# Products of probabilities and values: the second head of a pair asked for first in each part

## The chip, the cores and the metric

The kernel runs on one core of a Trainium2 chip. The metric is the device time of one execution in microseconds (us). TensorE does the matrix products (PE in the profile's lines, with PEld for its loads of the stationary operand), VectorE is DVE, ScalarE is ACT, GpSimd is POOL and SyncE is SP.

## What is computed

One layer of a decoder with 256 tokens and a model width of 2048, all in float32: a norm, one input projection that feeds three kinds of attention (dilated windows "a", block-sparse "b", and "c" with compressed, selected and window branches), the output projection, a second norm, and a feed-forward block with a short convolution. What the change touches is the last step of every attention head, the product of its probabilities with its values:

```python
p, lse = masked_softmax(s, mask)
o = jnp.einsum('bdhnqk,bdhnke->bdhnqe', p.astype(v.dtype), vb)          # mixer a
o_s = jnp.einsum('bkgqs,bkqse->bkgqe', p_s.astype(v_slc.dtype), vs)     # mixer c, selected
o_w = jnp.einsum('bkgqs,bkse->bkgqe', p_w.astype(v_win.dtype), vw)      # mixer c, window
return g[..., 0:1] * o_c + g[..., 1:2] * o_s + g[..., 2:3] * o_w
```

There are 12 heads in a, 8 in b and 12 in c, each 64 wide. In c every head has a selected and a window branch with probabilities of their own, so there are 44 sets of probabilities in all.

## The kernel before

**Stages.** First come the input projections (`fm_unit` and `tm_group`), with the attention mixed in, then the output projection (the loops from L690 and L701), then the up projection (L751, 88 units) and the down projection (L765). Weights come from memory by SyncE's queue (L120); ScalarE makes their high part `wh` (L122) and VectorE the rest `wl` (L124). `product` multiplies both with the activations on TensorE: L182 streams 512 columns with `wh`, L186 streams 256 columns with `wl`.

**Attention as side work.** Each kind of attention is a Python generator. `step()` (L651) advances it between pieces of the projections, so the program order mixes both. That order is not yet the order on the engines: the kernel is built with `schedule_with_timeline_sim=True` (L861), and a planner then puts each engine's instructions into an order of its own, by program order and by its own estimates of when each operand will be there. Instructions that write the same tile keep their program order in it.

**One set of probabilities** (`pipeline`, L595). `scores` (L502) is on TensorE and `softmax` (L516) on VectorE and ScalarE; `scale` (L554) multiplies by the factors; `turn` (L558) transposes three blocks on TensorE (L560 to L562) into `pt`, and ScalarE copies them to `pts` (L564). After every second set, `values(a, b)` (L566) is called for the pair: `a` is the first and `b` the second head, and the turn of `a` stands ahead of that of `b` in the program.

**The pair's products** (`values`). Both heads write one PSUM tile `o`: `a` its partitions 0 to 63, `b` its partitions 64 to 127 (`half`, L304). The stationary operand is a block of values of 64 columns, which the trace shows as `128*64`, while projections and transposes are `128*128`. In a and b a pair has three parts of 128 columns. In c it has two parts, of 128 and 256 columns, for each of the two branches; the first branch starts `o` with a product of the compressed branch (L572), the second ends it. Each `T.matmul` in float32 at L580 or L572 shows as two loads and two matmuls in the trace. In all there are 22 calls: 12 in c, 6 in a, 4 in b. When a tile is complete, `keep` (L584) copies it out (L591, L592) and frees `o`, of which there is one.

In what follows a0, a1 (and a2) are the parts of the first head, b0, b1 (and b2) those of the second.

Of the kernel before, what the change touches and what calls it, by code (L numbers as in the profile page):

```python
# [89 lines left out]
def trunk(ctx, tc, xT, wfm, wtm, wout, wup, wdown, w1, w2, pe, relT, convp, onehot, maskc, cmask, vbmask, out):  # L90
# [116 lines left out]
    with tc.tile_pool(name="sc", bufs=2, space=bass.MemoryType.PSUM) as scp, \  # L207
# [96 lines left out]
        def half(i):  # L304
            return slice(64 * i, 64 * i + 64)
# [260 lines left out]
        def values(a, b):  # L566

            if st.get("o") is None:
                st["o"] = opp.tile([P, 512], F32, name="o")
                if a.group in "sw":  # L570
                    p = (a.h - 20) // 2
                    T.matmul(st["o"][:, :S], cmp["vb"][p // 4][:, p % 4, :], cmp["pc"][p // 4], start=True, stop=False)  # L572
            lo, hi = slice(0, P), slice(P, S)
            if a.group in "sw":
                parts = ((1, hi, slice(S, 384), False, False), (0, slice(0, S), slice(0, S), False, a.group == "w"))
            else:
                parts = ((0, hi, hi, True, False), (1, hi, slice(S, 384), False, True), (0, lo, lo, True, True))
            for kt, cols, src, start, stop in parts:
                for n in (a, b):
                    T.matmul(st["o"][half(n.hf), cols], vt[n.v][:, kt, n.col:n.col + HD], n.ts[:, src], start=start, stop=stop)  # L580
            if b.done is not None:
                keep(b.done)

        def keep(tile_i):  # L584
            o = st["o"]
            if 6 <= tile_i < 10:
                t = ap.tile([P, 2, S], F32R, name=f"ob{tile_i}", tag=("vc", "va0", "va1", "ob")[tile_i - 6])
            else:
                t = oo[0][:, tile_i if tile_i < 6 else tile_i - 4]
            oparts[tile_i] = t  # L590
            A.copy(t[:, 0, :], o[:, :S])  # L591
            V.tensor_tensor(t[:, 1, :], o[:, :S], t[:, 0, :].bitcast(F32), ALU.subtract)  # L592
            st["o"] = None

        def pipeline(insts, late, after):  # L595

            n = len(insts)
            for j in range(n + late + 2):
                ahead(insts, j)
                i = j - late - 1  # L600
                if 0 <= i < n and i % 2 == 1:
                    values(insts[i - 1], insts[i])
                if 0 <= j - late < n:
                    turn(insts[j - late])
                if j < n:
                    scores(insts[j])
                    softmax(insts[j])
                    after(j)
                yield
# [91 lines left out]
        for o in range(NK):  # L701
# [3 lines left out]
            for i in range(4):  # L705
                a, b = (t[:, (o % 2 * 4 + i) * P:(o % 2 * 4 + i + 1) * P] for t in w)
# [10 lines left out]
    for o in range(NK):  # L717
        for c in range(0, NF, 8):
            n = min(8, NF - c)
# [3 lines left out]
    with tc.tile_pool(name="act", bufs=1) as fp, tc.tile_pool(name="frot", bufs=2) as rp, \  # L723
# [41 lines left out]
        for o in range(NK):  # L765
            ps = fps.tile([P, 512], F32, name="up")
            for c in range(0, NF, 8):
                n = min(8, NF - c)
# [105 lines left out]
```

## Time and profile before

| what | us |
|---|---|
| median of three runs | 1191.85 |
| lowest and highest run | 1191.47 and 1200.58 |
| the profiled execution | 1195.29 |
| span of its instructions | 1193.5 |

The profiled execution took 1.8 us more than its span. The page of the profile gives busy times of the engines, groups of instructions and waits. The timeline lists instructions in order of time: the start, how long the row lasts, engine, line, operation, output and inputs, shapes and the number of merged instructions. Matmuls overlap in it, so the distance from one start to the next is what a matmul costs.

### The profile page before, as it was taken

Reading aid. Unit: us, or ns where it says so; the run is one execution under the profiler, and the core shown is the slowest. Engines: PE = TensorE matmul, PEld = TensorE weight load, DVE = VectorE, ACT = ScalarE, POOL = GpSimd, SP = SyncE. Lnnn points to the kernel's source line nnn. Section 1 sums busy time; section 2 is a strip of 40 time slices with the busy share of each in tenths; the row PEclk is TensorE's granted clock in tenths of the full one; section 3 lists DMA queues with packets and bytes.
Section 4 is the critical chain, followed back from the end, with each engine's and each line's share of the span. In section 5 each row is a group of like instructions: output and inputs, shape, how many; then the busy total and the mean of one; then the engine's idle time right before and its main releaser. Section 6 shows DMA issues by size and latency. Waiting matters only on the chain.

```text
span 1193.5 us, 18698 instructions
## 1 busy us (share of the span) xinstructions
PE 1168.9 (98%) x6874; PEld 1022.8 (86%) x6874; DVE 862.4 (72%) x1635; ACT 670.6 (56%) x1153; POOL 83.6 (7%) x105
## 2 busy tenths in 40 slices
PE   7999999999999999999999999999999999999996
PEld 6898888888888898888888888888888888888886
DVE  7867987767686696888888878878878655454443
ACT  6465787766774455655556555555555544444441
POOL 7400000100000090000000000000000000000000
PEclk9989999999999998999999999999999999999998
DMA  8575445556455754555555555555555666666661
GB/s 263 176 241 183 126 125 158 139 177 199 149 164 150 220 169 166 193 192 188 187 193 190 184 192 191 187 189 192 188 190 187 182 184 184 188 184 191 186 185 71
DMA packets 66795, 214.91 MB, mean 180 GB/s; under 512 B 7584, under 2 KB 10416, under 8 KB 66704
## 3 DMA queue, kind: packets, MB, share of 16 engines
q1 hardware_dynamic: 64896, 209.19, 54.8%
q0 software_dynamic: 1808, 4.53, 2.0%
q8 instruction: 54, 0.88, 0.3%
q14 instruction: 37, 0.30, 0.1%
HBM read 211.55 MB, written 2.15 MB: 179 GB/s over the span
## 4 chain that ended last, share of the span: by engine, by line
PE 91%; POOL 5%; DMA 2%; DVE 1%; issue 0%; ACT 0%; SPq 0%; DVEq 0%; POOLq 0%
PE up L182 39%; PE up L186 20%; PE mm L182 12%; PE mm L186 6%; PE o L580 2%; PE mm L386 2%; PE mm L385 2%; PE mm L387 2%; POOL ssq L242 1%; POOL ssq L170 1%; POOL sq L168 1%; PE sc L509 1%; DMA w1t<-in_w_dram 1%; DMA raw<-in_wfm_dram 1%; PE pt L560 1%; DMA gx<-in_xT_dram 1%
## 5 line engine op out<-in xcount | busy, mean ns | idle before, releaser
L124 DVE TENSOR_TENSOR wl<-raw,wh 128x1024 fp32r<-128x1024 f32 (+4 forms) x411 | 485.8, 1184 | 196.2 <-ACT wh L122 187.5
L122 ACT CAST wh<-raw 128x1024 fp32r<-128x1024 f32 (+4 forms) x411 | 411.2, 1001 | 284.8 <-PE up L182 192.5
L182 PE MATMUL up<-xx,wh 128*128 128x512 f32 x1408 | 486.2, 394 | 0.0
L186 PE MATMUL up<-xx,wl 128*128 128x256 f32 x1408 | 380.8, 281 | 0.0
L182 PEld LDWEIGHTS up<-xx,wh 128*128 128x128 f32 x1408 | 259.1, 188 | 51.4
L186 PEld LDWEIGHTS up<-xx,wl 128*128 128x128 f32 x1408 | 266.5, 189 | 7.9
L182 PE MATMUL up<-aa,wh 128*128 128x512 f32 x660 | 230.7, 393 | 0.0
L186 PE MATMUL up<-aa,wl 128*128 128x256 f32 x660 | 184.1, 283 | 0.0
L182 PE MATMUL mm<-xx,wh 128*128 128x512 f32 x448 | 161.5, 400 | 4.5 <-ACT wh L122 4.5
L182 PEld LDWEIGHTS up<-aa,wh 128*128 128x128 f32 x660 | 123.0, 188 | 27.3
L186 PE MATMUL mm<-xx,wl 128*128 128x256 f32 x448 | 124.6, 288 | 3.7 <-DVE wl L124 3.7
L186 PEld LDWEIGHTS up<-aa,wl 128*128 128x128 f32 x660 | 124.1, 188 | 1.4
L203 ACT COPY low<-up 128x256 f32<-128x256 f32 x88 | 32.7, 372 | 130.0 <-PE up L182 127.3
L182 PEld LDWEIGHTS mm<-xx,wh 128*128 128x128 f32 x448 | 84.0, 190 | 19.8 <-ACT wh L122 4.5
L186 PEld LDWEIGHTS mm<-xx,wl 128*128 128x128 f32 x448 | 85.5, 191 | 7.9 <-DVE wl L124 4.9
L204 DVE TENSOR_TENSOR low<-up,low 128x256 f32<-128x256 f32 x88 | 37.3, 424 | 57.0 <-ACT low L203 57.0
L182 PE MATMUL mm<-oo,wh 128*128 128x512 f32 x192 | 67.7, 399 | 0.0
L738 ACT ACTIVATE acc<-u,cw 128x256 f32<-128x256 f32 x88 | 53.2, 605 | 3.3 <-DVE u L736 0.6
L186 PE MATMUL mm<-oo,wl 128*128 128x256 f32 x192 | 52.0, 284 | 0.0
L386 PE MATMUL mm<-wh,xx 128*128 128x384 f32 (+2 forms) x128 | 46.2, 361 | 0.0
L387 PE MATMUL mm<-wl,xx 128*128 128x384 f32 (+2 forms) x128 | 46.1, 362 | 0.0
L385 PE MATMUL mm<-wh,xx 128*128 128x384 f32 (+2 forms) x128 | 46.0, 360 | 0.0
(206 smaller groups left out, 1263.6 us busy)
## 6 DMA issues: line engine op xcount, KB each, us to landing
raw<-in_wup_dram SPq DMA_DIRECT2D x176, 512.0 KB, 4.1
raw<-in_wdown_dram SPq DMA_DIRECT2D x80, 512.0 KB, 3.7
raw<-in_wfm_dram SPq DMA_DIRECT2D x62, 512.0 KB, 4.5
raw<-in_wo_dram SPq DMA_DIRECT2D x32, 384.0 KB, 3.1
raw<-in_wtm_dram SPq DMA_DIRECT2D x16, 384.0 KB, 3.5
bias<-table POOLq DMA_DIRECT2D x32, 128.0 KB, 3.7
raw<-in_wtm_dram SPq DMA_DIRECT2D x8, 512.0 KB, 4.5
raw<-in_wo_dram SPq DMA_DIRECT2D x8, 512.0 KB, 4.2
```

Of the source, the lines that this page charges most:

```text
L122: A.copy(wh[:, :n], raw[:, :n])
L124: V.tensor_tensor(wl[:, :n], raw[:, :n], wh[:, :n].bitcast(F32), ALU.subtract)
L168: G.tensor_tensor(tmp, x[:, o, :], x[:, o, :], ALU.mult)
L182: T.matmul(ps, a, m.rearrange("p c s -> p (c s)"), start=start, stop=stop)
L186: T.matmul(ps[:, :S], b, m[:, 0, :], start=False, stop=False)
L203: A.copy(t, ps[:, S:])
L204: V.tensor_tensor(t, ps[:, :S], t, ALU.add)
L385: T.matmul(pss[tt][:, :n], xx[:, kt, 0, ts], a, start=kt == 0, stop=False)
L386: T.matmul(pss[tt][:, :n], xx[:, kt, 1, ts], a, start=False, stop=False)
L387: T.matmul(pss[tt][:, :n], xx[:, kt, 0, ts], b, start=False, stop=kt == NK - 1)
L580: T.matmul(st["o"][half(n.hf), cols], vt[n.v][:, kt, n.col:n.col + HD], n.ts[:, src], start=start, stop=stop)
L738: A.activation(acc, u[:, 2:], AF.Identity, bias=cw[:, n, 3:4], scale=cw[:, n, 0:1])
```

## The change

In each part of `values`, the product of the second head `b` is written ahead of that of the first head `a`. Nothing is added or removed; the operands, the flags and the number of instructions stay.

```diff
@@ -576,7 +576,7 @@
             else:
                 parts = ((0, hi, hi, True, False), (1, hi, slice(S, 384), False, True), (0, lo, lo, True, True))
             for kt, cols, src, start, stop in parts:
-                for n in (a, b):
+                for n in (b, a):
                     T.matmul(st["o"][half(n.hf), cols], vt[n.v][:, kt, n.col:n.col + HD], n.ts[:, src], start=start, stop=stop)
             if b.done is not None:
                 keep(b.done)
```

## Rows read from the trace of the kernel before

**Rows 1.** The page, busy time of each engine, its share and instructions.

```profile
PE 1168.9 (98%) x6874; PEld 1022.8 (86%) x6874; DVE 862.4 (72%) x1635; ACT 670.6 (56%) x1153; POOL 83.6 (7%) x105
```

**Rows 2.** Busy time in three stretches: length, engines, PE's clock, DMA share, GB/s.

```profile
0.00:85.00 85.00, 74.28 (x399) 65.35 (x400) 64.31 (x92) 49.38 (x86) 36.53 (x42) 0.96 0.70 229
85.00:400.00 315.00, 315.00 (x1922) 268.66 (x1921) 240.02 (x716) 207.08 (x468) 15.56 (x29) 1.00 0.54 158
400.00:1193.50 793.50, 779.64 (x4557) 688.83 (x4555) 558.04 (x828) 414.12 (x600) 31.50 (x34) 0.99 0.57 183
```

**Rows 3.** Waits of PE: line, releaser, us in total, times, longest.

```profile
PE mm L186 <- DVE wl L124: 3.7, 4, 1.6
PE mm L146 <- POOL ssq L170: 2.7, 1, 2.7
```

**Rows 4.** Source line L580: loads for b (ns least/median/most), idle load path before all.

```profile
L580 PEld LDWEIGHTS o<-pts,v_b x48: 132/137/138, 350.3 to 372.3; 128*64 128x64 f32 x48
...
issue: 5.6, 21
```

**Rows 5.** Timeline of PE, a pair of b whose products stand in two places.

```profile
357.94 0.40 PE L182 MATMUL mm<-oo,wh 128*128 128x512 f32 x1
358.27 0.43 PE L580 MATMUL o<-pts,v_b 128*64 128x128 f32 x2
358.63 0.33 PE L560 MATMUL pt<-ident,p 128*128 128x128 f32 x1
...
359.37 0.28 PE L186 MATMUL mm<-oo,wl 128*128 128x256 f32 x1
359.58 0.87 PE L580 MATMUL o<-pts,v_b 128*64 128x128 f32 x10
360.38 0.50 PE L182 MATMUL mm<-oo,wh 128*128 128x512 f32 x1
```

**Rows 6.** Timeline of PE, the last pair of b, in one place, after projection products.

```profile
371.37 0.40 PE L182 MATMUL mm<-oo,wh 128*128 128x512 f32 x1
371.60 0.28 PE L186 MATMUL mm<-oo,wl 128*128 128x256 f32 x1
371.81 0.88 PE L580 MATMUL o<-pts,v_b 128*64 128x128 f32 x12
372.62 0.50 PE L182 MATMUL mm<-oo,wh 128*128 128x512 f32 x1
```

**Rows 7.** Timeline of PE, window branches of c: second stretch of one pair, another pair whole.

```profile
149.73 0.86 PE L580 MATMUL o<-pts,v_c 128*64 128x128 f32 x6
150.53 0.38 PE L507 MATMUL sc<-k,q 128*128 128x256 f32 x1
...
185.27 0.87 PE L580 MATMUL o<-pts,v_c 128*64 128x128 f32 x8
186.07 0.33 PE L560 MATMUL pt<-ident,p 128*128 128x128 f32 x1
```

**Rows 8.** Timeline of PE, c's selected branch: L572 by itself, and ahead of its pair.

```profile
137.22 0.59 PE L572 MATMUL o<-cvals 128*128 128x256 f32 x2
137.65 0.27 PE L560 MATMUL pt<-ident,p 128*128 128x128 f32 x1
...
156.68 0.60 PE L572 MATMUL o<-cvals 128*128 128x256 f32 x2
157.21 0.87 PE L580 MATMUL o<-pts,v_c 128*64 128x128 f32 x8
158.01 0.38 PE L507 MATMUL sc<-k,q 128*128 128x256 f32 x1
```

**Rows 9.** Timeline of ACT, the copy of the second head's probabilities for rows 5.

```profile
355.81 0.46 ACT L564 COPY pts<-pt 128x384 f32<-128x384 f32 x1
```

**Rows 10.** First and last short stretch of L580 but those of rows 5, PE's timeline.

```profile
138.30 0.43 PE L580 MATMUL o<-pts,v_c 128*64 128x128 f32 x2
...
365.31 0.43 PE L580 MATMUL o<-pts,v_b 128*64 128x128 f32 x2
```

## Prediction

> **What bounds the kernel now.** I read the page's first section, then the busy times by stretch, then PE's waits. PE is busy for 98% of the span [rows 1], but a busy PE is not a bound by itself, so the stretches count. [...] PE's idle time lies at the start (10.7 of the first 85 us) and behind 400 us (13.9 of 793.5) [rows 2]. Its waits for `wl` come to 3.7 us in four times and, as PE is never idle between 85 and 400 us, none of them is there [rows 3]. So from 85 to 400 us every 0.1 us that PE's stream loses or gains moves all that follows: what is shortened there must show in the end, unless it opens a wait.
>
> The next question is what L580 costs PE in that stretch. The source view of the line shows that the load path stood idle before L580's loads, for 5.6 us in 21 places under "issue" alone [rows 4]. The timeline tells why. From one L182 to the next instruction is usually 0.23 us (371.37 to 371.60) [rows 6]. From an L182 to an L580 behind it, it is 0.33 (357.94 to 358.27) [rows 5], so 0.10 us go on entering the form `128*64`. A stretch of two L580 instructions then takes 0.36 us to the next instruction (358.27 to 358.63), but a stretch of ten only 0.80 (359.58 to 360.38) [rows 5] and one of twelve 0.81 (371.81 to 372.62) [rows 6]. A stretch has a fixed price, and in a long one the two halves of the columns run side by side.
>
> **Which pairs stand in two places.** In rows 5 the two instructions at 358.27 are a0 alone, and the ten at 359.58 are b0, a1, b1, a2, b2. In rows 6 all twelve are together. I went through the timeline of the 22 pairs: 13 have a0 alone, at 138.3, 146.1, 158.4, 170.1, 191.8 (behind an L572), 202.8, 211.2 (likewise) and 217.9 us in c, at 248.2 and 301.8 in a, and at 350.3, 358.3 and 365.3 in b; the other 9 are whole. The first and the last short stretch beside rows 5 are in [rows 10], and all but the two behind an L572 look the same. That makes 22 + 13 = 35 stretches of L580.
>
> The planner causes this, not the chip: at 358.27 the probabilities of the second head had long been copied (355.81 + 0.46 = 356.27) [rows 9]. In the planner's own estimate a0 can go and b0 can't yet; so it issues a0, then other products, then b0 and all that stands behind it in the tile's program order.
>
> **The change part by part.** It removes no instruction and no DMA: 216 matmuls at L580 before and after, and no queue of SP or POOL gets another order by the text of the change.
>
> 1. *b0 becomes the head of the pair.* It needs the later probabilities, and a0 stands behind it in the order of `o`. So a0 can no longer go early, and when b0 goes, the copy for a0 lies behind it in time too. The 13 short stretches go.
> 2. *Price of one short stretch:* 0.36 us and 0.10 for entering = 0.46 us.
> 3. *What the moved product costs in its new place.* In b and a the stretch of ten becomes one of twelve: 0.80 against 0.81 us [rows 5, 6]. In c's window branch the stretch of six becomes one of eight: 0.80 (149.73 to 150.53) against 0.80 (185.27 to 186.07) [rows 7]. So it costs 0.01 us at most by these rows; I take 0.01. They show the same work with `a` in front; with `b` in front the halves only change places. If a0 did not run beside anything, the bound would be the two loads it brings, 2 x 0.137 = 0.27 us [rows 4]; the other bound is 0. I take the end that the rows show.
> 4. *L572.* In c's selected branch it stays first and needs neither head's probabilities, so it may now be issued early and stand alone in any of the six selected pairs. Alone it takes 0.43 us to the next instruction (137.22 to 137.65) and the pair then enters anew for 0.10, 0.53 in all; in front of its pair it is 0.53 (156.68 to 157.21) [rows 5, 8]. I take nothing. The last two pairs of c read 64 rows in it, without a row of a lone one; by the price of one short stretch each way, two of them can't move the sum by more than 0.9 us, which the range holds.
> 5. *What is late next.* a0 ends later, but the last product of a pair, which releases `keep`, stands where it stood. The wait for b0 is not new: b0 headed the second stretch before, and in rows 5 its probabilities were there 3.3 us before its start (356.27 to 359.58) [rows 5, 9]. Behind b0 in PE's queue stand the projection products, so a late b0 would hold them all; that is the rival below.
>
> The sum: 13 x (0.46 - 0.01) = 5.9 us off PE's stream, 3.6 of it in c, 0.9 in a and 1.4 in b. The weights must follow: DVE needs 240.0 us for what would then take 309.1 instead of 315 [rows 2], 78% instead of 76%, which leaves it room. Behind 400 us the squares on POOL (L170) hold PE for 2.7 us [rows 3], but they begin only when the output projection's sums are there, so they move with PE.
>
> [...]
>
> **The rivals.**
>
> *A. The moved product is paid in its new place.* Each pair gains 0.46 - 0.27 = 0.19 us, 13 x 0.19 = 2.5 us: 1189.4 us on the median. Against it stand the equal stretches of rows 5 to 7; for it only that no row shows `b` in front. [...]
>
> *B. The change does not do what it says.* The planner could part the pair elsewhere, after b0 say, when its estimate of the next product is late. Then 13 stretches come back in another form, and the time stays at 1191.9 us. Against it: behind b0 no pair is parted now; the rest is always in one piece.
>
> *C. b0 holds PE (slower).* With a0 gone from the front there is nothing of the pair to run while the second copy is awaited. If the planner's order brought b0 so early that PE waited for one copy of 0.46 us [rows 9] in each of 22 pairs, the loss would be 10.1 us, and 1191.9 - 5.9 + 10.1 = 1196.1 us the time. It decides from 0.27 us of waiting per pair (5.9 / 22). Against it: the margin is 3.3 us in rows 5.
>
> *D. The planner's whole order shifts.* Where one product moves, its estimates of everything behind move, and transposes, scores and weight splits can change places. A worse order could add waits like the 3.7 us for `wl` [rows 3], which gives 1186.0 + 3.7 = 1189.7, twice that 1193.4; a better one could take as much off, 1182.3 or less. Nothing in the rows tells the sign; PE without any idle time and DVE at 76% speak for small effects.
>
> **How the numbers follow.** The profiled execution took 1195.29 us, 1.8 around its span of 1193.5 included; there the sum gives 1189.4. The median of the runs is 3.4 us below it, and the gain doesn't hang on what sets these runs apart: 1191.85 - 5.9 = 1186.0 us. Chances: the forecast 0.70 (1184 to 1188), A 0.07, B 0.07, C 0.04, D to the worse 0.07 and to the better 0.05. The range reaches from 1181, below D's better case, to 1192.5, which takes in A, B and the first step of D; about 0.1 is left out, at C and the far ends of D. About 1% (12 us) is what a measurement of this kernel can tell from no change; the forecast of 0.5% lies within it. Faster by over 1% (below 1179.9) needs D twice over, 0.04; slower by over 1% (above 1203.8) needs C with twice its stall or D at its worst, 0.03; within 1% 0.93.
>
> **What would show it right or wrong.** In the timeline after, no stretch of two L580 instructions stands alone, and there are 22 stretches instead of 35, of 8 or 12 instructions each. In the source view of L580 the idle time under "issue" and its count fall by about a third. PE's idle time from 85 to 400 us stays at nothing, and the work of that stretch ends about 5.9 us earlier, with what follows as long as before. Long stretches of 1.0 us or more to the next instruction would show A; short ones left over would show B; waits of L580 for `pts` L564 in PE's idle time would show C; new waits for `wh`, `wl` or other tiles would show D, and then the prediction is wrong by their sum.

## The result

| | before | after |
|---|---|---|
| median of 20 runs, us | 1196.57 | 1190.35 |
| lowest and highest, us | 1191.47 and 1202.69 | 1185.33 and 1193.95 |
| profiled execution, us | 1195.29 | 1189.61 |

The ratio of after to before is 0.9942 (95% interval 0.9929 to 0.9954): 0.6% or 6.9 us faster (the two medians lie 6.2 us apart). That is clear of the noise of 20 runs, although the prediction took about 1% for what a measurement of this kernel can tell from no change.

The busy times of after in the same stretches as [rows 2] (length, PE, PEld, DVE, ACT, POOL, clock, DMA share, GB/s):

```profile
0.00:85.00 85.00, 74.68 (x383) 65.82 (x384) 62.97 (x91) 48.52 (x85) 36.86 (x42) 0.92 0.71 229
85.00:400.00 315.00, 315.00 (x1960) 272.80 (x1959) 242.72 (x721) 210.21 (x471) 15.55 (x29) 1.00 0.56 161
400.00:1187.90 787.90, 773.96 (x4535) 683.97 (x4533) 555.89 (x824) 412.57 (x598) 31.49 (x34) 0.99 0.57 184
```

PE is still never idle from 85 to 400 us, and more instructions fit in: 1960 instead of 1922. DVE is at 77%. The three longest waits of PE in after (line, releaser, us, times, longest) are below. The first, for the first weights, was 4.5 us in before; the other two stand in [rows 3]. As PE is never idle between 85 and 400 us, no wait lies there:

```profile
PE mm L182 <- ACT wh L122: 4.4, 1, 4.4
PE mm L186 <- DVE wl L124: 3.1, 3, 1.4
PE mm L146 <- POOL ssq L170: 2.7, 1, 2.7
```

The pair that is the third of b, in after's timeline of PE. In before it stood in two places, at 365.3 [rows 10] and 366.6 us:

```profile
363.38 0.28 PE L186 MATMUL mm<-oo,wl 128*128 128x256 f32 x1
363.59 0.88 PE L580 MATMUL o<-pts,v_b 128*64 128x128 f32 x12
364.40 0.33 PE L560 MATMUL pt<-ident,p 128*128 128x128 f32 x1
```

All twelve instructions are in one place, 0.81 us to the next instruction, as for the whole pair in [rows 6]. After's timeline has 22 stretches of L580, twelve of 8 and ten of 12 instructions, and no short one. The source view of L580 in after, idle time of the load path before its loads (us, times):

```profile
issue: 2.7, 10
ACT pts L564: 0.8, 3
```

With five single ones behind these there are 18 places and 4.6 us, where before had 33 places and 8.7 us, "issue" in [rows 4] among them. "issue" alone fell by half, and not by the third that was forecast. The three places under `pts` are not waits for the copies: by the timelines of ACT and PE the second head's copy had ended at least 2.9 us before the start of each of the 22 stretches.

**Where the time went.** Two points can be found in every trace: the 153rd L186, which lies ahead of the first scores (L507), and the first L191, in the output projection's second loop. Between them lies all that the change touches: ahead of the first point and behind the second, PE's instructions come in the same order of lines in before, in after and in every kernel of the experiments. PE's timeline, first of before, then of after:

```profile
99.48 0.28 PE L186 MATMUL mm<-xx,wl 128*128 128x256 f32 x1
...
413.29 0.28 PE L191 MATMUL mm<-ob,wh 128*128 128x256 f32 x1
```

```profile
102.29 0.28 PE L186 MATMUL mm<-xx,wl 128*128 128x256 f32 x1
...
409.41 0.28 PE L191 MATMUL mm<-ob,wh 128*128 128x256 f32 x1
```

The stage took 313.81 us before and 307.12 after: 6.7 us less. The rest of the profiled difference is not the change's. After reached the first point 2.8 us later, and what follows the second was 1.7 us shorter (780.2 to 778.5). At both places PE's granted clock was 0.50 for a while, for a length that differs between executions: ahead of the first point for 6.8 us in before and for 3.4 and 10.2 us in after, near 450 us for 6.8 us in before and for 3.4 in after. The mean clock in the two stretches, of before, then of after:

```profile
40.00:90.00 50.00, 47.62 (x267) 43.44 (x266) 35.25 (x71) 30.48 (x57) 5.66 (x7) 0.93 0.66 216
...
440.00:460.00 20.00, 17.28 (x85) 14.88 (x84) 11.06 (x15) 8.90 (x11) 9.42 (x12) 0.83 0.50 169
```

```profile
40.00:90.00 50.00, 47.76 (x249) 43.51 (x248) 32.14 (x60) 29.20 (x56) 5.22 (x7) 0.86 0.62 205
...
440.00:460.00 20.00, 17.29 (x92) 14.98 (x92) 10.92 (x17) 8.82 (x11) 5.78 (x9) 0.91 0.57 185
```

50 x 0.07 = 3.5 us lost and 20 x 0.08 = 1.6 us won by the clock are near the 2.8 and 1.7. So 2.8 - 6.7 - 1.7 = -5.6 us, the difference of the spans.

### The profile page after: what moved, and what is told of

It reads as the page before. It is cut to its first block, busy times and chain, and to the rows that moved or that the text cites. A ratio compares the mean times of both kernels' runs of the same rounds, so it can differ in the third digit from the quotient of the medians.

```text
span 1187.9 us, 18694 instructions
## 1 busy us (share of the span) xinstructions
PE 1163.6 (98%) x6874; PEld 1022.6 (86%) x6874; DVE 861.6 (73%) x1635; ACT 671.3 (57%) x1153; POOL 83.9 (7%) x105
## 4 chain that ended last, share of the span: by engine, by line
PE 91%; POOL 5%; DMA 2%; DVE 1%; issue 0%; ACT 0%; SPq 0%; DVEq 0%; POOLq 0%
PE up L182 40%; PE up L186 20%; PE mm L182 12%; PE mm L186 6%; PE mm L387 2%; PE mm L385 2%; PE mm L386 2%; PE o L580 1%; POOL ssq L242 1%; POOL ssq L170 1%; POOL sq L168 1%; PE sc L509 1%; DMA w1t<-in_w_dram 1%; DMA raw<-in_wfm_dram 1%; PE pt L422 1%; PE pt L560 1%
## 5 line engine op out<-in xcount | busy, mean ns | idle before, releaser
L186 PE MATMUL up<-xx,wl 128*128 128x256 f32 x1408 | 380.2, 280 | 0.0
L186 PEld LDWEIGHTS up<-xx,wl 128*128 128x128 f32 x1408 | 266.0, 189 | 7.9
L186 PE MATMUL up<-aa,wl 128*128 128x256 f32 x660 | 184.1, 283 | 0.0
L186 PE MATMUL mm<-xx,wl 128*128 128x256 f32 x448 | 125.2, 289 | 3.1 <-DVE wl L124 3.1
L186 PEld LDWEIGHTS up<-aa,wl 128*128 128x128 f32 x660 | 124.1, 188 | 1.4
L186 PEld LDWEIGHTS mm<-xx,wl 128*128 128x128 f32 x448 | 86.5, 193 | 7.0 <-DVE wl L124 4.4
L186 PE MATMUL mm<-oo,wl 128*128 128x256 f32 x192 | 51.7, 282 | 0.0
```

The costliest lines, as they stand in the source:

```text
L186: T.matmul(ps[:, :S], b, m[:, 0, :], start=False, stop=False)
```

## Experiments

The theory is that of places: each separate stretch of L580 has a price on PE, and the time follows their number. Its rivals are that the order of the halves is worth something in itself, and that the planner's other moves made the gain. Seven kernels tell them apart. Since the clock at the start moves a run by some us (2.8 between the two profiled executions above), three measures stand side by side in the table: the stage between the two points in the profiled execution; the median over runs of span times mean granted clock (the length at full clock, if all work slowed with it), less 1181.6 us, its value in 50 runs of before; and the ratio of times with its interval (20 runs of the change, 6 of together and of together_all, 10 to 12 of the others).

| kernel | stretches of L580 | stage against before, us | span x clock against before, us | ratio (95%) |
|---|---|---|---|---|
| before | 35 | 0 | 0 | 1 |
| the change | 22 | -6.69 | -6.5 | 0.9942 (0.9929 to 0.9954) |
| swap_c | 27 | -3.93 | -3.5 | 0.9983 (0.9971 to 0.9995) |
| swap_ab | 30 | -2.66 | -2.1 | 0.9986 (0.9968 to 1.0004) |
| turn_b_first | 22 | -5.45 | -6.6 | 0.9964 (0.9949 to 0.9979) |
| turn_b_first_swap | 36 | +0.57 | +1.1 | 0.9999 (0.9985 to 1.0013) |
| heads_apart | 22 | -4.20 | -4.2 | 0.9973 (0.9957 to 0.9988) |
| together | 16 | -8.70 | -8.7 | 0.9935 (0.9911 to 0.9960) |
| together_all | 12 | -10.04 | -10.0 | 0.9912 (0.9890 to 0.9935) |

### The change in c alone, and in a and b alone

```diff
-                for n in (b, a):
+                for n in (b, a) if a.group in "sw" else (a, b):
```

Expected of swap_c: 

> The second head stands first only in c (12 of the 22 calls); a and b keep the order of before. Theory of places: the time follows the number of separate stretches of L580 on TensorE. The order built here has 27 (35 before, 22 after the change), all 8 short ones of c are gone, and the 6.7 us that TensorE's stream gained between the first attention work and the end of the output projection come to 0.51 us for each of the 13: 8 x 0.51 = 4.1 us faster than before, a ratio near 0.9966. Rival of the halves (it is the order of the two column halves itself that is worth something, in each call): 12/22 x 6.9 = 3.8 us, hardly to be told apart by time here. Rival of a shifted order (the gain comes from other work that the planner moved): no tie to 8 of 13, so anything from 0 to 7 us.

```diff
-                for n in (b, a):
+                for n in (a, b) if a.group in "sw" else (b, a):
```

Expected of swap_ab: 

> The second head stands first only in a and b (10 of the 22 calls). Theory of places: 30 stretches of L580 in the order built, 5 fewer than before: 5 x 0.51 = 2.6 us faster than before, a ratio near 0.9979, and with the run of c alone the two gains add up to that of the whole change. Halves: 10/22 x 6.9 = 3.1 us. Shifted order: no tie, and the two gains need not add up.

The two points, in PE's timeline of swap_c, then of swap_ab:

```profile
105.87 0.28 PE L186 MATMUL mm<-xx,wl 128*128 128x256 f32 x1
...
415.75 0.28 PE L191 MATMUL mm<-ob,wh 128*128 128x256 f32 x1
```

```profile
101.26 0.28 PE L186 MATMUL mm<-xx,wl 128*128 128x256 f32 x1
...
412.40 0.28 PE L191 MATMUL mm<-ob,wh 128*128 128x256 f32 x1
```

309.88 and 311.14 us: 3.93 us less than before for 8 stretches fewer, 2.66 less for 5, so 0.49 and 0.53 us for each, against 0.51 for the whole change. Both add up to 6.59 of 6.69 us. By span times clock the gains are 3.5 and 2.1 us, which add up to 5.6 of 6.5. The ratios say less: 0.17% and 0.14% add up to about half of the change's 0.58%; the interval of swap_c leaves out the 0.9966 of the theory by a little, and that of swap_ab holds 1. The profiled execution of swap_c reached the first point 6.4 us later than that of before, in work that no edit touches. A shifted order has no reason to add up like this in the stage; the halves are not excluded yet.

### Which head's probabilities come last

```diff
-                if 0 <= j - late < n:
-                    turn(insts[j - late])
+                if 0 <= j - late < n and (j - late) % 2 == 1:
+                    turn(insts[j - late])
+                    turn(insts[j - late - 1])
```

Expected of turn_b_first, this edit on the kernel before: 

> The products keep the order of before (first head first), but the turns of a pair are swapped: both in the second head's step, the second head's ahead of the first's, so that the first head's probabilities now come last. Theory of places: the head of the pair waits for the last probabilities, as in the change, and the order built has 22 stretches: about 13 x 0.51 = 6.7 us faster than before, a ratio near 0.9944, with 1 to 2 us to either side for the later turn of the first head. Halves: the second head is not in front, so the time of before, ratio 1.000. Shifted order: no tie to the 6.7.

Expected of turn_b_first_swap, this edit on the changed kernel: 

> The turns of a pair are swapped as in the run before, and the products too, as in the change: the second head is in front again, but its probabilities now come first. Theory of places: the head of the pair goes early by itself; the order built has 36 stretches, 14 of them short: 0.5 us slower than before, a ratio near 1.0004, and 7.2 us slower than the run with the turns alone. Halves: the gain of the change stays, ratio near 0.994. Shifted order: no tie.

The two points in turn_b_first, then in turn_b_first_swap:

```profile
106.29 0.28 PE L186 MATMUL mm<-xx,wl 128*128 128x256 f32 x1
...
414.65 0.28 PE L191 MATMUL mm<-ob,wh 128*128 128x256 f32 x1
```

```profile
103.14 0.28 PE L186 MATMUL mm<-xx,wl 128*128 128x256 f32 x1
...
417.52 0.28 PE L191 MATMUL mm<-ob,wh 128*128 128x256 f32 x1
```

308.36 and 314.38 us. With the order of before, but the first head's probabilities last, the stretches fall to 22 and the gain comes, although `b` is nowhere in front. Its stage holds one loss of its own, a piece at low clock (turn_b_first, busy times by stretch):

```profile
126.00:130.00 4.00, 4.00 (x17) 3.55 (x16) 2.27 (x6) 0.00 (x0) 0.00 (x0) 0.57 0.46 153
```

4 x (1 - 0.57) = 1.7 us; without it the stage would be 7.2 us shorter than before. The ratio of times, 0.9964 (0.9949 to 0.9979), stays behind the 0.9944 of the theory; the mean granted clock of its runs is lower than that of before's (0.9875 against 0.9887), and by span times clock the gain is 6.6 us. With `b` in front and its probabilities first, 14 short stretches come back and the gain is gone: +0.57 us in the stage, 0.9999 in time. The theory of the halves, which wanted 1.000 and 0.994 here, falls. So does that of a lucky order: of the stage's 1696 instructions outside L580, about 1540 keep before's order in the change, 1370 in turn_b_first and 1430 in turn_b_first_swap, and the time follows the stretches.

### How far the halves run side by side

```diff
-            for kt, cols, src, start, stop in parts:
-                for n in (b, a):
+            for n in (b, a):
+                for kt, cols, src, start, stop in parts:
```

Expected of heads_apart: 

> The change, but with all parts of the second head written ahead of all parts of the first, so the two column halves no longer take turns in the program order. The order built has 22 stretches of L580, as with the change, so the theory of places alone gives the change's time. What is tested is how far the halves run side by side. If they do so only for neighbours in the order, a pair of a or b takes about 0.16 + 10 x 0.109 + 0.20 = 1.45 us instead of 0.81 and one of c some 0.5 us more than its 0.80: 10 x 0.64 + 12 x 0.5 = 12.4 us slower than the change, 5.7 us slower than before, a ratio near 1.005. If each half has its own way through the array whatever the order (or if they never ran side by side), the change's time stays, a ratio near 0.994, and the stretches stay at 0.80 us to the next instruction.

A pair of b and a pair of c in PE's timeline of heads_apart:

```profile
352.54 1.14 PE L580 MATMUL o<-pts,v_b 128*64 128x128 f32 x12
353.62 0.50 PE L182 MATMUL mm<-oo,wh 128*128 128x512 f32 x1
...
145.40 0.88 PE L580 MATMUL o<-pts,v_c 128*64 128x128 f32 x8
146.21 0.38 PE L507 MATMUL sc<-k,q 128*128 128x256 f32 x1
```

Neither theory had it. In c the four instructions of one head stand ahead of the four of the other, and a stretch still takes 0.81 us: its first two instructions start 13 ns apart, against 7 ns in the change. The records don't name the half of an instruction; it is inferred here from the order that the program asks for and from the spacing of the starts. In a and b six stand ahead of six, and a stretch takes 1.08 us instead of 0.81: two instructions run alone (from 352.54 and from 352.70 us), and only at 352.81 do two start together. 10 x 0.27 = 2.7 us, and the stage is 2.5 us longer than the change's. So the halves do run side by side beyond their neighbours, but only up to some distance, between four and six instructions here; and had they never done so, every stretch would be longer than 0.81 (1.45 us for one of twelve, by the estimate in the expectation).

### Fewer places still

In together, the selected branch's products of a pair of c wait for those of the window branch and follow them:

```diff
...
-                    values(insts[i - 1], insts[i])
+                    if insts[i].group == "s":
+                        held.append((insts[i - 1], insts[i]))
+                    else:
+                        values(insts[i - 1], insts[i], *held)
+                        held.clear()
...
-            for kt, cols, src, start, stop in parts:
-                for n in (b, a):
...
+            for pair in ((a, b),) + more:
+                for kt, cols, src, start, stop in parts:
...
+                    for n in pair[::-1]:
...
-            n.ts = rp.tile([P, 384], F32, name="pts", bufs=4)
+            n.ts = rp.tile([P, 384], F32, name="pts", bufs=6)
```

Expected of together: 

> The change, and in c the products of a pair's selected branch are held back and issued behind those of its window branch, in one place, with six buffers for the turned probabilities instead of four. The order built has 16 stretches, 6 fewer than the change. Theory of places: 6 x 0.51 = 3.1 us faster than the change, 19 x 0.51 = 9.7 us faster than before, a ratio near 0.992. Rival of held buffers: the selected branch's probabilities stay longer in their buffers and the tile o is copied out later by one stretch; if turns or projections wait for that, the gain is lost and TensorE shows waits between 85 and 400 us.

In together_all the test also holds back the first of two pairs of a or b; the second is then written to columns 0 to 255 of `o`, the one held back to columns 256 to 511:

```diff
-                    if insts[i].group == "s":
+                    if insts[i].group == "s" or insts[i].group in "ab" and i % 4 == 1 and i + 2 < n:
```

Expected of together_all: 

> As the run named together, and in a and b every two pairs of heads share one tile o (columns 0 to 255 and 256 to 511), so that their products stand in one place too, the later pair's first. The order built has 12 stretches, 10 fewer than the change. Theory of places: 10 x 0.51 = 5.1 us faster than the change, 23 x 0.51 = 11.7 us faster than before, a ratio near 0.990. Rival of held buffers: what is held longer (probabilities, the tile o until two copies are out) opens waits on TensorE, and the time falls short of that of the run named together or comes out above it.

The two points in together, then those of together_all with two of its pairs of b in one place (the product has line L585 there):

```profile
100.90 0.28 PE L186 MATMUL mm<-xx,wl 128*128 128x256 f32 x1
...
406.00 0.28 PE L191 MATMUL mm<-ob,wh 128*128 128x256 f32 x1
```

```profile
98.67 0.28 PE L186 MATMUL mm<-xx,wl 128*128 128x256 f32 x1
...
361.31 1.53 PE L585 MATMUL o<-pts,v_b 128*64 128x128 f32 x24
362.77 0.39 PE L186 MATMUL mm<-oo,wl 128*128 128x256 f32 x1
...
402.44 0.28 PE L191 MATMUL mm<-ob,wh 128*128 128x256 f32 x1
```

305.10 and 303.77 us. Both are faster than the change in the stage, by 2.0 us for 6 stretches and by 3.3 us for 10, where 3.1 and 5.1 were expected. No wait was opened: PE is busy for 315 of 315 us from 85 to 400 us in both. The price was mis-sized instead, since 0.51 us is that of a short stretch, and those were gone. A short stretch is also work that runs beside nothing: its two instructions start 0.16 us apart, where those of a whole stretch start in pairs, 7 ns apart. Two whole stretches of twelve take 2 x 0.81 = 1.62 us, one of twenty-four 1.46 (361.31 to 362.77); with one way in (0.10) and one way out (0.10, below) less, that is 0.36 us, and 10 x 0.36 = 3.6 us, near the 3.3. together_all has the best time of all, in six runs: 0.9912 of before, with an interval that overlaps the change's at its edge (0.9929 to 0.9935); the stage of the profiled execution and span times clock put it 3.3 and 3.5 us below the change.

## Why the prediction was right

**The bound.** PE's stream from 85 to 400 us set the time, and what was taken from it showed at the end: 6.7 us of the stage, 6.9 by the ratio.

**b0 as head, the 13 short stretches.** As forecast: all are gone, and 22 are left. turn_b_first shows that this, and not the place of the halves, is the cause; swap_c and swap_ab show it in parts. What the planner estimated, no run shows; the traces show the orders that it built.

**The price of one.** The mechanism was right and the size a little low, 0.45 us forecast against 0.51. The term that was missing is the way out: the first product behind a stretch is longer too. Before's timeline, behind the short stretches at 138.30 [rows 10] and 358.27 [rows 5]:

```profile
138.66 0.39 PE L186 MATMUL mm<-xx,wl 128*128 128x256 f32 x1
138.88 0.40 PE L182 MATMUL mm<-xx,wh 128*128 128x512 f32 x1
...
358.80 0.27 PE L561 MATMUL pt<-ident,p 128*128 128x128 f32 x1
358.91 0.27 PE L562 MATMUL pt<-ident,p 128*128 128x128 f32 x1
```

The L186 there takes 0.22 us to the next instruction; the usual one, over all of before's attention, takes 0.12. L560 takes 0.17 (358.63 to 358.80), its neighbour L561 0.11. Of the 13 short stretches 8 are followed by another product and 5 by L560: 8 x 0.10 + 5 x 0.06 = 1.1 us. The sum would have been 7.0 us, 0.3 above the 6.7 measured. The step that failed is item 2, which counted the way into the form `128*64` and the stretch, but not the way back.

**The moved product.** Free, as taken from the rows: the stretches keep 0.80 and 0.81 us with `b` in front. Rival A, which wanted 0.27 us more in each, falls; heads_apart adds that the halves stay side by side even when they are not neighbours. Both halves use all 128 rows, and their twelve instructions take 0.81 us, half of what the twelve loads alone would take one behind the other (12 x 0.137 = 1.64 us, by the median load in [rows 4]).

**L572.** Nothing, as taken: its 12 instructions and the way to the next take 3.26 us in before's stage and 3.25 in after's, summed from start to start, though two more of its pairs stand alone now.

**What is late next.** No wait for the copies (rival C): the least time between a second head's copy and the stretch that needs it was 2.9 us. No new wait for weights or other tiles (rival D), no pair parted in a new way (rival B).

**The time itself.** 1186.0 was forecast and 1190.35 measured. That lies outside the 1184 to 1188 to which the prediction gave 0.70, and nearer to the times of rival A (1189.4) and of rival D (1189.7); it is the trace, and not the time, that tells them apart. The miss has little to do with the change: the three runs of before that the forecast started from lay low (1191.85 against 1196.57 for 20), which is 4.7 us and more than the whole miss. From 1196.57 the same sum gives 1190.7. The forecast's own ratio, 0.9951, is 0.0009 above the measured one. That the profiled execution took 1189.61 us, where the sum gave 1189.4, is luck: the stage gave 0.8 us more than the sum, and what lies outside it took 1.1 us back (2.8 - 1.7).

## What to carry to other kernels

Where small products in another tile form are scattered through a stream that bounds the kernel, count the places (0.51 us for each short one here) and not the instructions, and read the price of a place from start to start, the way in and the way out included. Where a planner builds the order, an operand that is ready early can cause such a place (36 stretches in turn_b_first_swap, 22 in turn_b_first); to ask first for the one that comes last keeps the group together, here at no cost that the trace shows. A gain of this size is best read between two points of the trace that enclose it, with the granted clock between them beside it, and not from whole runs.

## What was not expected of the hardware

By the starts in heads_apart the two halves of 64 columns seem to have taken their matmuls out of program order: with four instructions of one half written ahead of four of the other they started 13 ns apart, with six ahead of six the second half started two instructions late. No run tells what sets this distance.

The clock made up most of the spread between runs. In the traces of before and after, PE's granted clock fell to 0.50 behind idle times near the start and near 440 us, for the lengths given above, and in turn_b_first inside a stage without idle time (0.57 from 126 to 130 us). The profiled executions of swap_ab and together had a mean clock of 0.992 over the span, against 0.990 in before and in after, though the load path waited for L170 in them as long as in before or longer (3.0 and 3.3 us against 3.0). Span times mean granted clock spread little: over 33 runs of before its mean is 1181.6 us with a standard deviation of 0.8 (a standard error of 0.13), while their times go from 1192.4 to 1202.3 with a standard deviation of 2.2. Why the clock fell from 126 to 130 us stays open.
